# A two-layer decoder trunk on one core: turned pieces of interleaved groups four steps apart

## The chip, the cores and the metric

The kernel runs on one core of one Trainium2 chip. The metric is the device time of one launch in microseconds, the median over runs; lower is better. Engines are named as in the profile: PE multiplies matrices, DVE does vector work, ACT applies functions and scaled copies, POOL and SP here mostly issue DMAs. DMAs are issued from the queues of SP, POOL and ACT, and each engine takes its instructions in order.

## The reference

The input x is 256 tokens by 2048 features, float32. Two layers follow each other, each a mixer and a gated feed-forward net (ffn) with a residual sum after both.

```python
h = rms_norm(x, gain)                                   # before every mixer and ffn
# layer 0, mixer A and B: one projection to u, v, q, f, i, g (1024 each)
u, v = gelu(u), rms_norm_per_head(gelu(v))              # 8 heads of 128
y_a  = u * (tril(sp_w) @ v + sp_b)                      # in chunks of 128 tokens
y_b  = rms_norm_per_head(hgrn2(q, f, i)) * silu(g)      # gated linear recurrence, 8 heads
x    = x + concat(y_a, y_b) @ w_out
# layer 1, mixer C: q, k, v, g (2048 each) and f (16)
q, k = rms_norm_per_head(q), rms_norm_per_head(k)       # 16 heads of 128
c    = cumsum(log_sigmoid(f + b_f))                     # one row of 256 per head
p    = softmax(causal(q @ k.T * 128**-0.5 + c_t - c_s))
x    = x + ((p @ v) * sigmoid(g)) @ w_out
# ffn in both layers, hidden size 5632
z    = causal_conv3(h @ w_up); a, b = split(z)
x    = x + (silu(a) * b) @ w_down
```

All products are to be good to float32.

## The kernel before

**Matmuls and weights.** A float32 product is made of three matmuls of rounded operands. An activation is kept as a rounded half and a rounded remainder side by side; a weight w arrives by a DMA of 512 KB on SP's queue (L195), ACT writes its rounded copy wh (L206) and DVE the remainder wl (L211). Then PE adds high by high (L287), high by low (L288) and low by high (L289), in `project_four`; `project_tok` does the same for weights laid out by token columns (L267 to L269). The contraction runs over 16 tiles of 128 features (KT = 16, "k-tiles"). One weight tile holds two k-tiles of a group of 512 columns; the 12 matmuls on it are called a step here, and a group takes eight steps. There are four w buffers and three each of wh and wl; the ffn has a second set of two each for every other weight.

**Order of the work.** The program is written as a main line of projections, with everything else in generators. `tick()` is called once ahead of every step and moves each running generator one piece on. `start(g)` runs a generator's first piece at once, `after(n, g)` lets it begin n ticks later, and `queue` holds those that wait until fewer than `depth` of its kind run. A scheduler then orders each engine's instructions by their dependences and this program order; some orders are pinned by hand (`behind`, `in_order`). SP's queue thus holds the weights in the order of the steps, with other DMAs in between.

**Turning.** Projections come out with tokens on the partitions. `transposed` (L308 to L314) turns a group of 512 columns: two DVE transposes into `tmp`, then 16 DMAs of 32 KB into the turned tile, eight on SP's queue and eight on POOL's. After a turn, LAG = 6 ticks pass before the result is used. These 32 KB DMAs are the "turned pieces" of a group, tiles `turn` or `zt` in the profile.

**Pairs.** Where a projection begins with activations that are not all ready, two groups are interleaved by `project_pair`, so that the first 12 k-tiles of both come before the last four of either (JOIN = 12):

```python
for part in ((0, JOIN), (JOIN, KT)):
    for w4, ps in ((wa, pa), (wb, pb)):
        project_four(w4, acts, KT, shift=shift, ps=ps, part=part)
```

In steps: a 6, b 6, a 2, b 2. It serves four places: the outputs of both mixers (`w_abo` with activations `ya` and `yb`, `w_co` with `yc`; two more groups follow alone) and the first two groups of `up` in both ffns.

**Mixer A and B.** `w_v` comes first: two groups, with the loads of x and the first norm between them. The sums of squares of the values v (`sumsq`, a mult L353 and a reduce L354 on DVE, four times), the reciprocal root (`rsq`, L345 to L350, with Ln and Exp on ACT) and four multiplies of gv (L495) are written right after the second group. `mixes`, in `queue`, then makes the eight spatial products, one per tick, after three empty ticks. The first x block, the vector pp and the second x block are issued by ACT's queue (`SC.dma_start`, L84 to L86) at the very start, while the first `w_v` parts are on SP's.

**Mixer C.** The first group of queries (`project_tok` on `w_cqkv[0]`) is interleaved with `keys_gate`, which makes the first group of keys and the 16 columns of the gate f in one pass: queries 12 k-tiles, keys 12, queries 4, keys 4. Then `forget` makes the cumulated gate rows: fc on 16 partitions (a scan, L804), written to DRAM as cd (L806) and read back into cb, every row on all partitions, by one POOL DMA of 2 MB (L807). The queries' and keys' `turn` does the norm per head (`sumsq`, `rsq`, a mult L883) and then `transposed`; both are begun by `start`. Attention reads cb and the turned tiles.

The profile's lines L335 and L714 are the first norm's rounded x tile `a` and the low half of a `yb` tile.

Of the kernel before, what the change touches and what calls it, by code (L numbers as in the profile page):

```python
# [8 lines left out]
F32 = mybir.dt.float32  # L9
# [6 lines left out]
P = 128  # L16
# [10 lines left out]
LAST = 7  # L27
WAIT = 2
JOIN = 12
EPS = 1e-6  # L30
WARM = 7
AHEAD = {2: 2, 4: 4, 6: 6}
# [21 lines left out]
def tile_trunk(ctx: ExitStack, tc: tile.TileContext, x, pp_d, cst_d, mlev_d, msk_d,  # L54
# [13 lines left out]
    def nm(base):  # L68
        count[0] += 1
        return f"{base}_{count[0]}"  # L70
# [13 lines left out]
    SC.dma_start(*fetch[0])  # L84
    SC.dma_start(pp[:, 0:C_FFN], pp_d[:, 0:C_FFN])
    SC.dma_start(*fetch[1])  # L86
    V.memset(ones, 1.0)
# [49 lines left out]
    def start(g):  # L137

        if next(g, g) is not g:
            free.append(g)  # L140
# [30 lines left out]
        while flight or queue or free or soon:  # L171
            tick()

    deep = {"pool": None, "turn": 0}

    def in_order(r, key="dma"):
        if key in deep:
# [98 lines left out]
    def project_four(w4, acts, n, k0=0, shift=0, ps=None, part=None):  # L276
        ps = ps or banks_for()
        for k in range(*(part or (0, n)), 2):
            tick()
            lo = (k0 + (k + shift) % n) * P  # L280
            wh, wl = weights(w4[:, :, lo:lo + 2 * P].rearrange("m p c -> p m c"), 1024, 4)
            for T in range(2):
                for i in range(2):
                    a = acts[k + i]
                    ah, al = a[:, T * P:(T + 1) * P], a[:, S + T * P:S + (T + 1) * P]
                    h, l = (view(t, i * P, (2 * P, 4), (1, P)) for t in (wh, wl))
                    PE.matmul(ps[T], ah, h, start=k + i == 0, stop=False)  # L287
                    PE.matmul(ps[T], ah, l, start=False, stop=False)  # L288
                    deep["mm"] = deep["main"] = PE.matmul(ps[T], al, h, start=False, stop=k + i == n - 1)  # L289
        return ps  # L290

    def project_pair(wa, wb, acts, shift=0):
        pa, pb = banks_for(), banks_for()
        for part in ((0, JOIN), (JOIN, KT)):
            for w4, ps in ((wa, pa), (wb, pb)):
                project_four(w4, acts, KT, shift=shift, ps=ps, part=part)
                if part[1] == KT:
                    yield ps

    def output(w, acts, shift=0):  # L300
        yield from project_pair(w[0:4], w[4:8], acts, shift)
# [38 lines left out]
    def rsq(dst, src, n):  # L340
        tag = "sq" if dst.shape[-1] == S else "rm"
        cols = dst.shape[-1] if dst.shape[-1] == S else LANE // math.prod(dst.shape[1:-1])
        m, t = (tp.tile(list(dst.shape[:-1]) + [max(cols, dst.shape[-1])], F32, tag=tag, name=nm(n_))
                [..., 0:dst.shape[-1]] for n_ in ("rm", "rt"))
        V.tensor_scalar(m, src, 1.0 / n, EPS, ALU.mult, ALU.add)  # L345
        act(dst, m, AF.Ln)
        act(dst, dst, AF.Exp, scale=-0.5)
        V.scalar_tensor_tensor(t, dst, -0.5, dst, ALU.mult, ALU.mult)
        V.tensor_tensor(t, t, m, ALU.mult)
        V.scalar_tensor_tensor(dst, t, 1.5, dst, ALU.add, ALU.mult)  # L350

    def sumsq(dst, src, sq):
        V.tensor_tensor(sq, src, src, ALU.mult)  # L353
        V.tensor_reduce(dst, sq.rearrange("p (h d) -> p h d", d=P), AX.X, ALU.add)  # L354
# [65 lines left out]
    def mixer_ab(norm):  # L420
# [61 lines left out]
                        .to_broadcast([P, NH, P]), ALU.mult)  # L482

        ss = hp.tile([P, LANE], F32, tag="ss", name="ss")
        for g in range(2):
            for T in range(2):
                i = (2 * g + T) * 4
                j = hp.tile([P, 512], F32, tag="smk", name=nm("junk"), bufs=1)
                sumsq(ss[:, i:i + 4], gv[g][:, T], j)
        rsq(ss[:, 0:2 * NH], ss[:, 0:2 * NH], P)  # L490
        for g in range(2):
            for T in range(2):
                i = (2 * g + T) * 4
                v4 = gv[g][:, T].rearrange("p (h d) -> p h d", d=P)
                V.tensor_tensor(v4, v4, ss[:, i:i + 4].unsqueeze(2).to_broadcast([P, 4, P]), ALU.mult)  # L495
        mg = [keep("mg") for _ in range(NH)]

        def mix(h):
# [9 lines left out]
                                   ALU.mult, ALU.add)  # L508

        def mixes():  # L510
            yield
            yield
            yield
            for h in range(NH):
                mix(h)
                yield

        queue.append(mixes())


        gam = pp[:, C_GAM:C_GAM + 3 * NH]
# [225 lines left out]
    def mixer_c(norm):  # L747
# [6 lines left out]
        def keys_gate(part):  # L754
            for k in range(*part):
                if k % 2 == 0:
                    tick()
                w = wp.tile([P, n], F32, tag="w", name=nm("w"), bufs=4)
                wh = wp.tile([P, n], F32R, tag="wh", name=nm("wh"), bufs=3)
                wl = wp.tile([P, n], F32R, tag="wl", name=nm("wl"), bufs=3)  # L760
                nc.gpsimd.dma_start(w[:, 0:CH], w_cf[:, k * P:k * P + CH])
                nc.sync.dma_start(w[:, CH:n], w_cqkv[CH // 4][:, k * 512:(k + 1) * 512])
                deep["act"] = SC.activation(wh, w, AF.Copy)
                deep["sub"] = V.tensor_tensor(wl, w, wh.bitcast(F32), ALU.subtract)
                a = norm.a[k]
                for T in range(2):
                    ah, al = a[:, T * P:(T + 1) * P], a[:, S + T * P:S + (T + 1) * P]
                    for j, (a_, t) in enumerate(((ah, wh), (ah, wl), (al, wh))):
                        begin, end = k + j == 0, k == KT - 1 and j == 2
                        PE.matmul(pa[T][:, 0:CH + S], a_, t[:, 0:CH + S], start=begin, stop=end)  # L770
                        deep["main"] = PE.matmul(pb[T][:, 0:S], a_, t[:, CH + S:n], start=begin, stop=end)  # L771

        first = banks_for()
        for part in ((0, JOIN), (JOIN, KT)):
            project_tok(w_cqkv[0], norm, ps=first, part=part)
            keys_gate(part)
        drain()
        depth[0] = 2
        Rt = norm.Rt
# [3 lines left out]

        ct = hp.tile([P, 2, 2 * CH], F32, tag="ct", name="ct")[..., 0:CH]
        cb = hp.tile([P, CH * S], F32, tag="big", name="cb").rearrange("p (h s) -> p h s", s=S)

        def forget():
            f, fa, fc, on = (hp.tile([P, S], F32, tag=t, name=t)[0:CH] for t in ("f", "fa", "fc", "on"))
            ft = hp.tile([P, 2, LANE], F32, tag="ft", name="ft")
            V.memset(on, 1.0)  # L790
            for T in range(2):
                SC.activation(ft[:, T, 0:CH], pa[T][:, 0:CH], AF.Copy, scale=Rt[:, T:T + 1])
            yield
            ps = bank()
# [8 lines left out]
            V.scalar_tensor_tensor(f, f, 0.0, fa, ALU.min, ALU.subtract)  # L803
            V.tensor_tensor_scan(fc, on, f, 0.0, ALU.mult, ALU.add)  # L804
            cd = dp.tile([CH, S], F32, tag="cd", name="cd")
            nc.gpsimd.dma_start(cd, fc)  # L806
            nc.gpsimd.dma_start(cb, cd.partition_broadcast(P))  # L807
# [82 lines left out]
        for g in range(CH // 4):  # L890
            qkv = []
            for j in range(3):
                ps = None if g == 0 and j == 1 else first if g + j == 0 else \
                    project_tok(w_cqkv[j * (CH // 4) + g], norm)
                z = piece("z", 2) if j < 2 else piece("v", 2)
                if ps is None:
                    start(forget())
                for T in range(2):
                    if ps is None:
                        SC.activation(z[:, T, 0:S], pa[T][:, CH:CH + S], AF.Copy, scale=Rt[:, T:T + 1])  # L900
                        SC.activation(z[:, T, S:512], pb[T][:, 0:S], AF.Copy, scale=Rt[:, T:T + 1])
                    else:
                        SC.activation(z[:, T], ps[T], AF.Copy, scale=Rt[:, T:T + 1])
                if j < 2:
                    t = piece("turn", 4)
                    start(turn(z, t))
                    z = heads(t)
                qkv.append(z)
            os_.append(piece("o", CH // 4))
            queue.extend(attend(h, *qkv, os_[g]) for h in range(4 * g, 4 * g + 4))  # L910
# [284 lines left out]
```

## Time and profile before

| | us |
|---|---|
| median of 3 runs | 2319.3 |
| lowest and highest run | 2317.0, 2320.3 |
| the profiled execution, device time | 2317.44 |
| its span in the profile | 2315.7 |
| PE busy | 2292.7 |
| DVE, ACT, POOL busy | 1557.9, 1313.3, 356.5 |

The span is the time from the first to the last recorded work of one execution; the device time of that execution is 1.7 us longer. Times inside the trace count from the start of the span. "Busy" for PE also counts matmuls at a reduced clock: the profile shows the granted clock as PEclk, where 1.00 is full speed. An instruction's row gives its start, its length, engine, line and operation, the tile written and the tile read (`pm<-wh,a`), and in brackets how long its engine stood idle before it and what ended that.

### The profile page before, as it was taken

To read this page: it belongs to the slowest core of one execution; us is meant where nothing else is said; L and a number is where in the kernel's file an instruction comes from. 1 tells how busy PE (TensorE), PEld (TensorE's weight loads), DVE (VectorE), ACT (ScalarE), POOL (GpSimd) and SP (SyncE) were. 2 spreads that over 40 slices of the span, in tenths; PEclk is the share of its full clock that TensorE was granted. 3 is DMA by queue.
4 is the path that set the end of the run, shared out by engine and by line. 5 is a ranking of instruction groups with operands and counts; after the bars stand their busy time and mean duration, and the time that the engine had idled before them with its cause. 6 is when DMAs were issued, how large, how long until landed. Compare 5 with 4: busy or idle time off the path is not lost.

```text
span 2315.7 us, 31427 instructions
## 1 busy us (share of the span) xinstructions
PE 2292.7 (99%) x10370; PEld 1903.9 (82%) x10370; DVE 1557.9 (67%) x2369; ACT 1313.3 (57%) x1953; POOL 356.5 (15%) x661
## 2 busy tenths in 40 slices
PE   9999999999999999999989999999999999999999
PEld 7888887888888888888868888878888888888887
DVE  7788766777566657766756665657777467657666
ACT  7577655665455545654545556646655456456642
POOL 0101121122012002111211101121221022012102
PEclk9999999999999999999999999999999999999999
DMA  8755667777667657776666555767777677667765
GB/s 273 205 186 169 187 204 222 228 235 214 203 204 218 214 185 227 221 215 189 181 198 201 185 187 174 227 207 229 235 219 219 193 213 218 204 203 219 220 204 172
DMA packets 499204, 481.06 MB, mean 208 GB/s; under 512 B 116992, under 2 KB 468368, under 8 KB 498912
## 3 DMA queue, kind: packets, MB, share of 16 engines
q1 hardware_dynamic: 475344, 451.83, 62.5%
q0 software_dynamic: 21248, 23.69, 4.6%
q10 hardware_dynamic: 2448, 3.53, 0.5%
q8 instruction: 81, 1.33, 0.2%
q14 instruction: 83, 0.68, 0.1%
HBM read 434.85 MB, written 2.12 MB: 189 GB/s over the span
## 4 chain that ended last, share of the span: by engine, by line
PE 75%; DMA 2%; DVE 1%; SPq 1%; issue 0%; ACT 0%; DVEq 0%; ACTq 0%; POOLq 0%
PE pm L288 21%; PE pm L289 21%; PE pm L287 21%; PE pm L267 3%; PE pm L268 3%; PE pm L269 3%; SPq L314 1%; DMA zt<-tmp 1%; PE px L161 1%; PE px L770 1%; DMA turn<-tmp 0%; PE pm L771 0%; DVE wl L211 0%; DVE tmp L308 0%; PE px L164 0%
## 5 line engine op out<-in xcount | busy, mean ns | idle before, releaser
L211 DVE TENSOR_TENSOR wl<-w,wh 128x1024 fp32r<-128x1024 f32 (+1 forms) x812 | 986.7, 1218 | 655.6 <-ACT wh L206 650.0
L206 ACT ACTIVATE wh<-w 128x1024 fp32r<-128x1024 f32 (+1 forms) x812 | 854.6, 1054 | 796.3 <-PE pm L289 555.6
L288 PE MATMUL pm<-wl,a 128*128 128x512 f32 x1792 | 698.4, 390 | 2.9 <-DVE wl L211 2.9
L287 PE MATMUL pm<-wh,a 128*128 128x512 f32 x1792 | 701.0, 391 | 0.0
L289 PE MATMUL pm<-wh,a 128*128 128x512 f32 x1792 | 698.1, 390 | 0.0
L314 POOL DMA_DIRECT2D zt<-tmp x413 | 223.7, 549 | 1203.0 <-DVE tmp L308 1000.6
L288 PEld LDWEIGHTS pm<-wl,a 128*128 128x128 f32 x1792 | 336.8, 188 | 73.3 <-DVE wl L211 4.6
L289 PEld LDWEIGHTS pm<-wh,a 128*128 128x128 f32 x1792 | 336.6, 188 | 69.8
L287 PEld LDWEIGHTS pm<-wh,a 128*128 128x128 f32 x1792 | 336.7, 188 | 69.2
L288 PE MATMUL pm<-wl,hid 128*128 128x512 f32 x688 | 267.9, 389 | 0.0
L287 PE MATMUL pm<-wh,hid 128*128 128x512 f32 x688 | 267.9, 389 | 0.0
L289 PE MATMUL pm<-wh,hid 128*128 128x512 f32 x688 | 267.9, 389 | 0.0
L314 POOL DMA_DIRECT2D turn<-tmp x224 | 121.4, 550 | 635.3 <-DVE tmp L308 299.1
L267 PE MATMUL pm<-wh,a 128*128 128x512 f32 x464 | 184.3, 398 | 8.3 <-ACT wh L206 8.3
L268 PE MATMUL pm<-wl,a 128*128 128x512 f32 x464 | 181.9, 392 | 0.2 <-DVE wl L211 0.2
L269 PE MATMUL pm<-wh,a 128*128 128x512 f32 x464 | 181.6, 391 | 0.0
L289 PEld LDWEIGHTS pm<-wh,hid 128*128 128x128 f32 x688 | 129.2, 188 | 26.8
L287 PEld LDWEIGHTS pm<-wh,hid 128*128 128x128 f32 x688 | 129.2, 188 | 26.7
L288 PEld LDWEIGHTS pm<-wl,hid 128*128 128x128 f32 x688 | 129.2, 188 | 26.7
L155 ACT ACTIVATE conv<-zt,pp 128x256 f32<-128x256 f32 x176 | 95.6, 590 | 24.2 <-DMA zt<-tmp 23.0
L267 PEld LDWEIGHTS pm<-wh,a 128*128 128x128 f32 x464 | 87.6, 189 | 26.0 <-ACT wh L206 8.7
L308 DVE STREAM_TRANSPOSE tmp<-z 128x512 f32<-128x512 f32 x132 | 92.2, 706 | 18.4 <-ACT z L974 16.0
(217 smaller groups left out, 1935.3 us busy)
## 6 DMA issues: line engine op xcount, KB each, us to landing
w<-in_w_up SPq DMA_DIRECT2D x352, 512.0 KB, 4.5
w<-in_w_dn SPq DMA_DIRECT2D x176, 512.0 KB, 4.3
w<-in_w_cqkv SPq DMA_DIRECT2D x88, 512.0 KB, 4.3
w<-in_w_abo SPq DMA_DIRECT2D x32, 512.0 KB, 4.4
w<-in_w_cg SPq DMA_DIRECT2D x32, 512.0 KB, 4.0
w<-in_w_co SPq DMA_DIRECT2D x32, 512.0 KB, 4.0
zt<-tmp SPq DMA_DIRECT2D x414, 32.0 KB, 2.4
zt<-tmp POOLq DMA_DIRECT2D x413, 32.0 KB, 2.3
```

The source lines that it names most:

```text
L155: return behind(SC.activation(*args, **kw), "act")
L161: return behind(PE.matmul(*args, **kw), "main")
L206: deep["act"] = SC.activation(wh[:, p], w[:, p], AF.Copy)
L211: deep["sub"] = V.tensor_tensor(wl[:, p], w[:, p], wh[:, p].bitcast(F32), ALU.subtract)
L267: PE.matmul(ps[T], ah, h, start=k + i == 0, stop=False)
L268: PE.matmul(ps[T], ah, l, start=False, stop=False)
L269: deep["main"] = PE.matmul(ps[T], al, h, start=False, stop=k + i == KT - 1)
L287: PE.matmul(ps[T], ah, h, start=k + i == 0, stop=False)
L288: PE.matmul(ps[T], ah, l, start=False, stop=False)
L289: deep["mm"] = deep["main"] = PE.matmul(ps[T], al, h, start=False, stop=k + i == n - 1)
L308: V.transpose(tmp.rearrange("p (b m i t) -> p b m i t", b=4, m=4, t=2)[:, :, :, :, T], src(T).rearrange("p (m b j) -> p b m j", m=4, b=4))
L314: qs[(a + b) % len(qs)].dma_start(dst[BLK * b:BLK * (b + 1), :, a * n:(a + 1) * n], tmp[BLK * a:BLK * (a + 1), b * 4 * n:(b + 1) * 4 * n] ...
```

## The change

It has six parts.

1. The first x block is issued by SP's queue, ahead of the first weights, and takes its place in the chain of pinned DMAs, instead of by ACT's queue.
2. `project_pair` gives the second group eight k-tiles at first (HALF = 8), not 12. In steps: a 6, b 4, a 2, b 4. Group a ends four steps ahead of group b, before it was two.
3. The start of mixer C does the same with the first queries and keys.
4. The values' sums, `rsq` and multiplies become steps of a generator, with a tick between them, and `mixes` goes on from there; it is begun by `after(6, ...)` and no longer counted in `queue`.
5. The gate rows cb are read back in four DMAs of four rows (512 KB) each, four ticks apart.
6. The turn of the first keys begins four ticks later.

```diff
+HALF = 8
...
-    SC.dma_start(*fetch[0])
+    first_dma = nc.sync.dma_start(*fetch[0])
...
-    deep = {"pool": None, "turn": 0}
+    deep = {"pool": None, "turn": 0, "dma": first_dma}
...
     def project_pair(wa, wb, acts, shift=0):
         pa, pb = banks_for(), banks_for()
-        for part in ((0, JOIN), (JOIN, KT)):
-            for w4, ps in ((wa, pa), (wb, pb)):
-                project_four(w4, acts, KT, shift=shift, ps=ps, part=part)
-                if part[1] == KT:
-                    yield ps
+        for w4, ps, part in ((wa, pa, (0, JOIN)), (wb, pb, (0, HALF)), (wa, pa, (JOIN, KT)), (wb, pb, (HALF, KT))):
+            project_four(w4, acts, KT, shift=shift, ps=ps, part=part)
+            if part[1] == KT:
+                yield ps
...
-        for g in range(2):
-            for T in range(2):
-                i = (2 * g + T) * 4
-                j = hp.tile([P, 512], F32, tag="smk", name=nm("junk"), bufs=1)
-                sumsq(ss[:, i:i + 4], gv[g][:, T], j)
-        rsq(ss[:, 0:2 * NH], ss[:, 0:2 * NH], P)
...
+        def values():
+            for g in range(2):
+                for T in range(2):
+                    i = (2 * g + T) * 4
+                    j = hp.tile([P, 512], F32, tag="smk", name=nm("junk"), bufs=1)
+                    sumsq(ss[:, i:i + 4], gv[g][:, T], j)
+                    yield
+            rsq(ss[:, 0:2 * NH], ss[:, 0:2 * NH], P)
+            for g in range(2):
+                for T in range(2):
...
+                    V.tensor_tensor(v4, v4, ss[:, i:i + 4].unsqueeze(2).to_broadcast([P, 4, P]), ALU.mult)
+                yield
...
         def mixes():
-            yield
-            yield
-            yield
+            yield from values()
             for h in range(NH):
                 mix(h)
                 yield
 
-        queue.append(mixes())
+        after(6, mixes())
...
         first = banks_for()
-        for part in ((0, JOIN), (JOIN, KT)):
+        for part, other in (((0, JOIN), (0, HALF)), ((JOIN, KT), (HALF, KT))):
             project_tok(w_cqkv[0], norm, ps=first, part=part)
-            keys_gate(part)
+            keys_gate(other)
...
+        def rows(to, of):
+            nc.gpsimd.dma_start(to, of)
+            yield
...
-            nc.gpsimd.dma_start(cb, cd.partition_broadcast(P))
+            for g in range(4):
+                c = slice(4 * g, 4 * g + 4)
+                after(4 * g, rows(cb[:, c], cd[c].partition_broadcast(P)))
...
-                    start(turn(z, t))
+                    if ps is None:
+                        after(4, turn(z, t))
+                    else:
+                        start(turn(z, t))
```

More of the change, by code (lines that the diff above doesn't have):

```diff
@@ L484, in mixer_ab @@
         ss = hp.tile([P, LANE], F32, tag="ss", name="ss")
-        for g in range(2):
-            for T in range(2):
-                i = (2 * g + T) * 4
-                j = hp.tile([P, 512], F32, tag="smk", name=nm("junk"), bufs=1)
-                sumsq(ss[:, i:i + 4], gv[g][:, T], j)
-        rsq(ss[:, 0:2 * NH], ss[:, 0:2 * NH], P)
[L491 to L495, printed above, removed]
+        def values():
[8 more added lines that the diff above has]
+                for T in range(2):
+                    i = (2 * g + T) * 4
+                    v4 = gv[g][:, T].rearrange("p (h d) -> p h d", d=P)
+                    V.tensor_tensor(v4, v4, ss[:, i:i + 4].unsqueeze(2).to_broadcast([P, 4, P]), ALU.mult)
+                yield
         mg = [keep("mg") for _ in range(NH)]
```

## The prediction

> **What bounds the kernel now.** I read the page's first part, then the windows for the places where PE falls behind, then PE's waits, and last the queues' own timelines there.
>
> ```profile
> span 2315.7 us, 31427 instructions
> PE 2292.7 (99%) x10370; PEld 1903.9 (82%) x10370; DVE 1557.9 (67%) x2369; ACT 1313.3 (57%) x1953; POOL 356.5 (15%) x661
> ```
>
> PE is busy for 99% of the span and the change takes no matmul away, so only PE's losses can be won. Busy time hides some of them: a matmul at half clock counts as busy. I therefore count matmuls against an undisturbed stretch (columns: stretch, length, busy us and number of each engine, granted clock, DMA share, GB/s).
>
> ```profile
> core 0: us, PE busy (x) PEld busy (x) DVE busy (x) ACT busy (x) POOL busy (x), PEclk, DMA share, GB/s
> 500.00:750.00 250.00, 250.00 (x1105) 207.10 (x1104) 160.09 (x209) 139.69 (x184) 39.01 (x72) 1.00 0.69 210
> 48.00:62.00 14.00, 12.83 (x56) 9.91 (x56) 12.73 (x27) 11.67 (x16) 1.05 (x1) 1.00 0.52 156
> 350.00:365.00 15.00, 12.48 (x47) 9.55 (x46) 8.14 (x15) 8.17 (x14) 0.00 (x0) 0.89 0.79 247
> 455.00:466.00 11.00, 10.27 (x45) 8.16 (x45) 11.00 (x22) 8.19 (x14) 4.00 (x8) 1.00 0.46 133
> 1180.00:1200.00 20.00, 11.69 (x39) 8.79 (x38) 7.53 (x14) 7.41 (x14) 2.97 (x6) 0.74 0.64 208
> 1550.00:1565.00 15.00, 13.12 (x50) 10.03 (x49) 7.08 (x13) 7.23 (x13) 1.86 (x4) 0.89 0.84 251
> 1558.30:1561.60 3.30, 3.30 (x9) 2.56 (x8) 3.10 (x6) 1.96 (x4) 0.00 (x0) 0.50 0.95 294
> ```
>
> 250/1105 = 0.2262 us is one matmul, and 12 of them, 2.72 us, one step (two k-tiles). A stretch's loss is its length less 0.2262 times its matmuls: 14 - 56 x 0.2262 = 1.3 at 48, 4.4 at 350, 0.8 at 455, 11.2 at 1180, 3.7 at 1550. (A few matmul records may be missing, so each is good to some tenths.) At 1558.3 the clock is 0.50 after a stall, so a stall costs more than its idle time.
>
> ```profile
> PE pm L267 <- ACT wh L206: 8.3, 1, 8.3
> 1556.73 0.50 PE L287 MATMUL pm<-wh,yc 128*128 128x512 f32 x1 [1.35 <-ACT wh L206]
> ```
>
> The largest wait, 8.3 us at once (total, times, longest), is for a rounded weight at 1180; of the 11.2 there the other 2.9 are half clock. ACT had nothing to round, as SP's queue and POOL's timeline show (start, us, instruction):
>
> ```profile
> 338.19 11.80 SPq L314 DMA_DIRECT2D turn<-tmp  x16
> 350.10 6.59 SPq L195 DMA_DIRECT2D w<-in_w_abo  x5
> 1168.65 16.12 SPq L314 DMA_DIRECT2D turn<-tmp  x16
> 1184.87 6.52 SPq L195 DMA_DIRECT2D w<-in_w_cqkv  x5
> 1540.46 11.16 SPq L314 DMA_DIRECT2D turn<-tmp  x16
> 1551.73 8.39 SPq L195 DMA_DIRECT2D w<-in_w_co  x6
> 1166.92 0.56 POOL L807 DMA_DIRECT2D cb<-cd  x1 [2.02 <-DMA cd<-fc]
> 1178.08 4.89 POOL L314 DMA_DIRECT2D turn<-tmp  x9 [5.38 <-DMA turn<-tmp]
> 1169.29 11.01 DMA turn<-tmp
> w<-in_w_cqkv SPq DMA_DIRECT2D x88, 512.0 KB, 4.3
> turn<-tmp SPq DMA_DIRECT2D x224, 32.0 KB, 2.1
> cb<-cd POOLq DMA_DIRECT2D x1, 2048.0 KB, 10.9
> ```
>
> SP issues in order, weights included. At 338, 1540 and 1168 two groups' turned pieces (8 + 8) stand back to back, and no weight is issued for 11.8, 11.2 and 16.1 us: more than four steps (10.9 us), what the four w buffers cover. At 1168 there is more: a piece took 11.01 us where the median is 2.1, beside the 2 MB gate rows, issued 1166.92 and 10.9 us long; SP and POOL stood behind it.
>
> **The change part by part.**
>
> *Outputs (w_abo, w_co).* The two interleaved groups end four steps apart, not two. In the changed order SP issues 8 pieces, three weights, 8 pieces. Half of 11.8 is 5.9 us, two steps, inside what four buffers cover. I take the stalls as gone but 0.2 each: -4.2 and -3.5 (ends: all gone, -4.4 and -3.7; nothing gained, 0). No DMA is added here. The first group's last four activations are wanted two steps earlier:
>
> ```profile
> L287 PE MATMUL pm<-wh,yb x64: 388/389/629, 309.4 to 390.0; 128*128 128x512 f32 x64
> L714 DVE SCALAR_TENSOR_TENSOR yb<-turn,pp,yb x16: 427/436/447, 287.4 to 313.4; 128x128 fp32r<-128x128 f32 x16
> ```
>
> In w_abo the yb tiles are the last eight of 16. The first group takes the first four in two steps from 309.4, the second group's four steps follow, and the last four are wanted at 309.4 + 6 x 2.72 = 325.7. The last is written at 313.4 + 0.4 = 313.8: 11.9 us spare, no cost.
>
> *Start of mixer C.* Queries and keys' groups also end four steps apart; the keys' turn comes four ticks later; the gate rows go in four DMAs. SP: 8 query pieces, five weights, 8 key pieces. POOL: 8 query pieces, the gate row's cd, two parts, 8 key pieces, two parts; so the query pieces pass ahead of the broadcast, and the key pieces meet 1 MB (half of 10.9, 5.4 us) instead of 2. The three added issues are 3 x 0.56 = 1.7 us of a POOL busy for 15%. The old 11.2 goes. What is late next is DVE: in the new order these stand between the third split (wl) and the fourth of the next group (durations from before, other order):
>
> ```profile
> 1162.14 0.40 DVE L803 SCALAR_TENSOR_TENSOR f<-f,fa 16x256 f32<-16x256 f32 x1
> 1162.47 0.67 DVE L353 TENSOR_TENSOR junk<-z 128x512 f32<-128x512 f32 x1
> 1163.14 0.67 DVE L804 TENSOR_TENSOR_SCAN fc<-on,f 16x256 f32<-16x256 f32 x1
> 1163.74 0.65 DVE L354 TENSOR_REDUCE ss<-junk 128x4 f32<-128x512 f32 x1
> 1165.80 0.17 DVE L345 TENSOR_SCALAR rm<-ss 128x8 f32<-128x8 f32 x1
> 1165.92 1.29 DVE L883 TENSOR_TENSOR z<-z,ss 128x512 f32<-128x512 f32 x2
> 1167.13 0.16 DVE L348 SCALAR_TENSOR_TENSOR rt<-ss 128x8 f32<-128x8 f32 x1
> 1167.20 0.70 DVE L308 STREAM_TRANSPOSE tmp<-z 128x512 f32<-128x512 f32 x1
> 1168.55 1.21 DVE L211 TENSOR_TENSOR wl<-w,wh 128x1024 fp32r<-128x1024 f32 x1
> ```
>
> 0.40 + 0.67 + 0.67 + 0.65 + 0.17 (rm), a round trip to ACT for Ln and Exp (rm to rt is 1.33 with mults between: I take 0.7), three small ones 0.5, 1.29, 0.70 and the split 1.21: 7.0, less some 0.4 because starts lie closer than durations: 6.6 us. The first split must end as the first step begins; up to the third stand two splits, a small add, one junk and one reduce, 2 x 1.21 + 0.17 + 0.67 + 0.65 = 3.9, so the fourth ends at 3.9 + 6.6 = 10.5. PE wants it after three steps and the fourth's first matmuls, 3 x 2.72 + 1.0 = 9.2. A new gap of 1.3, then; the nearest row is 1.35 at 1556.73, followed by half clock over 3.3 us, which costs half of that, 1.6. New loss 2.9, net -8.3. Ends: 0 (sums run ahead; -11.2) and 8.2 (gap doubled to 2.6; two late parts make the next weight 2.7 late, half of 5.4; half clock 2.9 as at 1180; -3.0). I take 2.9 because the broadcast's late parts have loaded weights ahead of them. [...]
>
> *up(0), both ffns.* The same turn; before, 0.8 is lost at 455 where the two groups' convolutions fill DVE (11.00 of 11). Four steps apart they overlap less, but fall among later ones: -0.4 (ends -0.8, +0.8).
>
> *Values' sums.* As generator steps they keep nearly their place on DVE; the rsq and the four multiplies go about 12 steps later, and ACT gets two more table loads:
>
> ```profile
> L97 ACT ACT_TABLE_LOAD x19 | 24.4, 1283 | 2.5 <-issue 2.1
> ```
>
> 2 x 1.28 = 2.6 us on an engine 57% busy, hidden by two waiting rounded tiles; multiplies of some 0.65 each join DVE later. The 1.3 at 48 comes from sums that stay. 0 (ends -1.3; +1.5, about one load uncovered).
>
> *First x block on SP instead of ACT.*
>
> ```profile
> 0.74 0.86 SPq L195 DMA_DIRECT2D w<-in_w_v  x2
> 0.73 0.42 ACTq L84 DMA_DIRECT2D x<-in_x  x1
> 1.18 0.45 ACTq L85 DMA_DIRECT2D pp<-in_pp  x1
> 5.23 0.35 DVE L335 TENSOR_SCALAR a<-x,pp 128x256 fp32r<-128x256 f32 x1 [4.22 <-DMA pp<-in_pp]
> ```
>
> ACT's pp goes 0.45 earlier and SP's weights 0.43 later. The first activation waits for pp, so it may gain, until the later weight takes over: -0.2 (ends -0.6, +0.2).
>
> Sum: -4.2 - 3.5 - 8.3 - 0.4 + 0 - 0.2 = -16.6. Against the profiled execution, 2317.4: 2300.8. That execution stands 1.9 below the median of 2319.3, so 2302.7 on the scale of the runs; I say 2302.5.
>
> **Rivals.**
>
> *Nothing new at mixer C's start.* DVE's sums fit between splits and the 11.2 goes whole: -4.2 - 3.5 - 11.2 - 0.6 = -19.5, 2299.8. For it: the scheduler may be run ahead by idle DVE (7.53 busy of 20 there). Against: DVE runs in order, and the round trip stands ahead of the fourth split.
>
> *A long new stall there*, the 8.2 above: -4.2 - 3.5 - 3.0 - 0.6 = -11.3, 2308.0. For it: a piece behind a broadcast took 11.01 us. Against: parts are a quarter as large, and weights stood on another queue. [...]
>
> *Pairs still late.* Three weights between two lots of pieces are too few, and both outputs keep their stalls: -8.3 - 0.6 = -8.9, 2310.4. For it: the weights that follow 1551.73 still take 8.39 for six. Against: 8 pieces are half the hole.
>
> *Slower: the earlier use of the last four activations.* In five places (both outputs, both up(0), mixer C's start) PE would reach acts 12 to 15 two steps, 5.4 us, earlier. If they come 3.0 late each time, each costs 3.0 and 1.6 of half clock: 23, and -16.6 + 23 = +6.4, 2325.7. From 2.6 late in all five it is slower by 0.2%. Against: by the rows above they would have to come 11.9 us later in w_abo to be late at all.
>
> **How the numbers follow.** Forecast 0.56, nothing new 0.17, long stall 0.13, pairs late 0.06, slower 0.08. A measurement of this kernel tells about 0.2% (4.6 us) from no change. Long stall and pairs late still lie beyond it (11.3 and 8.9); to mixtures of them, with part of the slower one, goes 0.06 within: faster 0.86, same 0.06, slower 0.08. The range: all terms at their best, -4.4 - 3.7 - 11.2 - 0.8 - 1.3 - 0.6 = -22.0, 2297.3, less the 2.3 by which the lowest run lies under the median: 2295; above, pairs late 2310.4 and a little run scatter: 2312.
>
> **What would show it.** In the windows about 350 and 1550 the lost time under 0.5 and a clock of 1.00; in SP's timeline `turn<-tmp x8` with weights between instead of x16. At mixer C's start no PE wait near 8 us, key pieces well under 11 us, four cb rows of 512 KB, and a gap of about 1.3 named for wl. At 48 and 455 no more than about today's losses; 21 table loads with no PE wait beside them. It is wrong if PE waits for yb, yc or A tiles, if weights still come late at the pairs, or if a broadcast part now holds weights.

## The result

The changed kernel takes 2304.7 us (median of 4 runs, 2301.5 to 2308.9) against 2318.2 for the kernel before; the ratio is 0.9944, 95% interval 0.9923 to 0.9964. Measured again beside other kernels it was 2306.4, ratio 0.9962 (0.9948 to 0.9976). The forecast was 2302.5 in a range of 2295 to 2312. The execution that was profiled, and that all rows of "after" below come from, took 2308.89, the slowest of the four. Line numbers are up to twelve higher than before (L206 is L207, L211 is L212), and some are the same (L308, L314).

First the page's span and busy times of the changed kernel:

```profile
span 2307.1 us, 31430 instructions
PE 2289.0 (99%) x10370; PEld 1899.5 (82%) x10370; DVE 1559.8 (68%) x2369; ACT 1313.3 (57%) x1955; POOL 358.3 (16%) x664
```

Then the windows at the places that the prediction named (columns as there), with two more, at 30 and 72:

```profile
30.00:40.00 10.00, 9.23 (x40) 7.01 (x39) 6.94 (x11) 5.68 (x11) 0.00 (x0) 1.00 0.72 231
48.00:62.00 14.00, 12.72 (x56) 9.84 (x55) 12.57 (x24) 11.49 (x13) 0.90 (x1) 1.00 0.46 142
72.00:76.00 4.00, 2.55 (x10) 1.58 (x9) 2.04 (x2) 2.11 (x2) 0.56 (x1) 1.00 0.94 229
350.00:365.00 15.00, 14.63 (x64) 11.76 (x64) 10.83 (x20) 8.62 (x14) 1.02 (x2) 1.00 0.76 229
455.00:466.00 11.00, 11.00 (x49) 8.93 (x48) 8.50 (x10) 4.67 (x6) 4.33 (x8) 1.00 0.84 229
1160.00:1172.00 12.00, 11.03 (x49) 8.57 (x48) 8.57 (x15) 4.43 (x6) 4.92 (x9) 1.00 0.76 260
1172.00:1190.00 18.00, 15.45 (x60) 12.03 (x59) 6.34 (x6) 7.87 (x9) 2.19 (x4) 0.91 0.92 287
1550.00:1565.00 15.00, 12.97 (x49) 9.99 (x48) 11.95 (x20) 10.51 (x16) 0.38 (x1) 0.89 0.85 251
```

Length less 0.2262 us for each matmul gives the lost time: 0.5 at 350 (4.4 before), none at 455 (0.8), 0.9 + 4.4 = 5.3 at mixer C's start (11.2), but 3.9 at 1550 (3.7), still 1.3 at 48, and two new losses, 1.7 at 72 and 1.0 at 30. The differences are -3.9, -0.8, -5.9, +0.2, 0, +1.7 and +1.0, together -7.7; 2317.4 - 7.7 = 2309.7, near the 2308.9 of this execution.

PE's timeline of the changed kernel at the remaining losses (start, us, instruction, in brackets the idle time and what ended it):

```profile
73.95 0.49 PE L288 MATMUL pm<-wh,a 128*128 128x512 f32 x1 [0.68 <-ACT wh L207]
1165.09 0.50 PE L269 MATMUL pm<-wl,a 128*128 128x512 f32 x1 [0.97 <-DVE wl L212]
1180.55 0.73 PE L268 MATMUL pm<-wh,a 128*128 128x512 f32 x2 [2.03 <-ACT wh L207]
1181.81 0.79 PE L269 MATMUL pm<-wl,a 128*128 128x512 f32 x1 [0.53 <-DVE wl L212]
1551.83 0.50 PE L288 MATMUL pm<-wh,yc 128*128 128x512 f32 x1 [1.28 <-ACT wh L207]
1553.09 0.50 PE L289 MATMUL pm<-wl,yc 128*128 128x512 f32 x1 [0.76 <-DVE wl L212]
```

The 8.3 us wait is gone. A gap of 0.97 for a split and a wait of 2.03 for a late weight stand in its place.

SP's timeline shows the two outputs side by side, and why one was mended and the other not:

```profile
335.54 5.10 SPq L314 DMA_DIRECT2D turn<-tmp  x8
340.74 1.63 SPq L196 DMA_DIRECT2D w<-in_w_abo  x3
346.42 5.11 SPq L314 DMA_DIRECT2D turn<-tmp  x8
...
1527.40 5.11 SPq L314 DMA_DIRECT2D turn<-tmp  x8
1532.62 2.79 SPq L196 DMA_DIRECT2D w<-in_w_co  x3
1541.20 5.10 SPq L314 DMA_DIRECT2D turn<-tmp  x8
1546.41 16.57 SPq L196 DMA_DIRECT2D w<-in_w_co  x9
```

In both, the second group's pieces come as eight after three weights. In w_abo they start 10.9 us after the first group's, in w_co 13.8. SP stands in order before 1541.20 and has nothing to issue, because tmp isn't turned yet. POOL's and DVE's timelines of the changed kernel tell why:

```profile
1531.68 2.71 POOL L314 DMA_DIRECT2D turn<-tmp  x5 [2.39 <-issue]
1540.12 0.43 DVE L159 TENSOR_TENSOR x<-x,turn 128x256 f32<-128x256 f32 x1 [2.99 <-DMA w<-in_w_co]
1540.46 0.71 DVE L308 STREAM_TRANSPOSE tmp<-z 128x512 f32<-128x512 f32 x1
```

After three of the first group's pieces POOL was held for 2.39 us by nothing that the profile names ("issue"). The other five pieces then went out together with three weights. DVE's first sum into x (L159), which needs all pieces of that group, waited 2.99 us, and behind it, in order, stood the second transpose of the second group. The row names a weight, which the sum doesn't read; the last of the five late pieces landed at 1539.55.

At mixer C's start the chain that ended last runs over two weights:

```profile
1165.06 7.22 DMA w<-in_w_cqkv
1174.73 4.63 DMA w<-in_w_cqkv
```

The first took 7.22 us (median of w_cqkv 4.4 in this kernel, 4.3 in the one before) beside two parts of the gate rows, and the next was issued only when that one had been rounded and split. By the prediction it should have been covered.

### The profile page after: what moved, and what is told of

The parts are those of the page before. It is cut to its first block, busy times and chain, and to the rows that moved or that the text cites. A ratio compares the mean times of both kernels' runs of the same rounds, so it can differ in the third digit from the quotient of the medians.

```text
span 2307.1 us, 31430 instructions
## 1 busy us (share of the span) xinstructions
PE 2289.0 (99%) x10370; PEld 1899.5 (82%) x10370; DVE 1559.8 (68%) x2369; ACT 1313.3 (57%) x1955; POOL 358.3 (16%) x664
## 3 DMA queue, kind: packets, MB, share of 16 engines
HBM read 434.85 MB, written 2.12 MB: 189 GB/s over the span
## 4 chain that ended last, share of the span: by engine, by line
PE 91%; DMA 4%; DVE 2%; ACT 2%; issue 1%; SPq 1%; POOL 0%; DVEq 0%; ACTq 0%
PE pm L289 26%; PE pm L290 25%; PE pm L288 25%; PE pm L269 4%; PE pm L270 4%; PE pm L268 4%; PE px L162 1%; DVE wl L212 1%; ACT wh L207 1%; DMA w<-in_w_cqkv 1%; DMA w<-in_w_abo 1%; DMA w<-in_w_f 1%; DMA w<-in_w_v 0%; DMA w<-in_w_co 0%; SPq L314 0%
## 5 line engine op out<-in xcount | busy, mean ns | idle before, releaser
L212 DVE TENSOR_TENSOR wl<-w,wh 128x1024 fp32r<-128x1024 f32 (+1 forms) x812 | 985.8, 1218 | 653.2 <-ACT wh L207 649.0
L207 ACT ACTIVATE wh<-w 128x1024 fp32r<-128x1024 f32 (+1 forms) x812 | 854.2, 1054 | 798.1 <-PE pm L290 563.2
L314 POOL DMA_DIRECT2D zt<-tmp x413 | 223.7, 549 | 1201.8 <-DVE tmp L308 993.9
L289 PEld LDWEIGHTS pm<-wl,a 128*128 128x128 f32 x1792 | 336.5, 188 | 74.1 <-DVE wl L212 5.1
L288 PEld LDWEIGHTS pm<-wh,a 128*128 128x128 f32 x1792 | 336.5, 188 | 70.4 <-ACT wh L207 1.1
L290 PEld LDWEIGHTS pm<-wh,a 128*128 128x128 f32 x1792 | 336.3, 188 | 70.1
L314 POOL DMA_DIRECT2D turn<-tmp x224 | 121.5, 550 | 634.1 <-DVE tmp L308 267.4
L269 PEld LDWEIGHTS pm<-wl,a 128*128 128x128 f32 x464 | 87.7, 189 | 23.1 <-DVE wl L212 5.7
L308 DVE STREAM_TRANSPOSE tmp<-z 128x512 f32<-128x512 f32 x132 | 92.3, 706 | 20.1 <-ACT z L986 18.1
```

The costliest lines, as they stand in the source:

```text
L207: deep["act"] = SC.activation(wh[:, p], w[:, p], AF.Copy)
L212: deep["sub"] = V.tensor_tensor(wl[:, p], w[:, p], wh[:, p].bitcast(F32), ALU.subtract)
L308: V.transpose(tmp.rearrange("p (b m i t) -> p b m i t", b=4, m=4, t=2)[:, :, :, :, T], src(T).rearrange("p (m b j) -> p b m j", m=4, b=4))
L314: qs[(a + b) % len(qs)].dma_start(dst[BLK * b:BLK * (b + 1), :, a * n:(a + 1) * n], tmp[BLK * a:BLK * (a + 1), b * 4 * n:(b + 1) * 4 * n] ...
```

## The experiments

Each ran beside the kernel before on the same chip, whose medians there were 2315.9 to 2317.0. The edits are shown shortened; a line in words stands for the code of that part in the diff above.

### The outputs' part alone

```diff
 before
+HALF = 8
-project_pair: wa 0-12, wb 0-12, wa 12-16, wb 12-16
+project_pair: wa 0-12, wb 0-8, wa 12-16, wb 8-16
```

> The kernel before with part 2 alone (project_pair: wa 12, wb 8, wa 4, wb 8 k-tiles). Theory: the late weights at both outputs come from two groups' pieces back to back on SP, so the loss about 350 us (4.4) falls under 1; at w_co it goes too unless POOL's hold of 2.2 to 2.4 us falls among the first group's pieces. That hold stood at POOL's 430th instruction in both profiles; without the added broadcast issues it should fall after the sixth of the first group's eight pieces, so that two pieces are late instead of five, and the loss at 1550 is 0 to 4. Mixer C's start keeps its 11 to 12. Time 2309 to 2314. Rival (the hold is chance): it falls elsewhere, and the loss at 1550 is under 1, 2309.

Measured: 2306.8 (2306.4 to 2307.2), ratio 0.9957 (0.9942 to 0.9972). That is 9.4 us under the kernel before, as much as the whole change gained when it was measured the second time (9.6). Windows and POOL's timeline of this kernel:

```profile
350.00:365.00 15.00, 14.79 (x66) 11.90 (x65) 11.97 (x22) 10.33 (x18) 0.00 (x0) 1.00 0.86 271
1172.00:1195.00 23.00, 16.30 (x67) 12.48 (x66) 8.18 (x16) 11.83 (x25) 4.58 (x9) 0.85 0.65 208
1545.00:1565.00 20.00, 19.05 (x84) 15.20 (x83) 15.11 (x25) 12.18 (x20) 3.28 (x7) 1.00 0.81 251
1532.39 1.09 POOL L314 DMA_DIRECT2D turn<-tmp  x2 [2.18 <-issue]
```

At 350 nothing is lost, and at 1550 only 20 - 84 x 0.2262 = 1.0, with the hold where the expectation put it, after the sixth piece: two pieces are late, not five. At mixer C's start 7.8 is still lost in the second window. Its time lies below the expected 2309 to 2314, since that loss and smaller ones also came out lower than in the profile of before; of these I have no cause.

### Mixer C's start alone

```diff
 before
+first queries and keys 12, 8, 4, 8 k-tiles
+cb in four DMAs, after(4 * g)
+first keys' turn by after(4)
```

> The kernel before with parts 3, 5 and 6 alone (mixer C's start). Theory: the wait of 8.3 goes and in its place come a DVE gap of about 1.0 and a late weight of 2 with half clock, as in the changed kernel's profile; loss between 1150 and 1200 some 7 instead of 12.6; outputs keep 4 to 5 each. Time 2311 to 2315. Rival (the new stalls there come from what the other parts delay): loss there under 3, 2308 to 2310.

Measured: 2310.7 (2307.9 to 2315.3), ratio 0.9975 (0.9965 to 0.9984). The new gaps at mixer C's start come with this part itself: PE waits 1.06 for a split, then 0.50, 0.53, 0.68 and 0.76 us for late weights and their splits between 1181 and 1187. The waits for late weights are smaller than in the changed kernel, and no half clock followed: the loss between 1160 and 1200 is 4.3, where some 7 was expected.

### Part 4 alone, and undone

```diff
 before
+values() in steps, mixes() by after(6)
```

> The kernel before with part 4 alone (values in steps, mixes by after). Theory: od is issued 1 to 2 us later against PE's work, its 11 to 13 us of slow transfers then reach into the next group's weights, and a loss of 2 to 5 us appears at 73 where the kernel before has none; everything else as before, 2317 to 2321. Rival (the loss at 73 needs the first x block on SP too): none at 73, 2315 to 2317.

Measured: 2319.5 (2313.4 to 2321.8), ratio 1.0009 (0.9999 to 1.0019): not told apart from no change by the interval, but the loss is there, in PE's timeline:

```profile
74.70 0.50 PE L287 MATMUL pm<-wh,a 128*128 128x512 f32 x1 [2.74 <-ACT wh L206]
```

```diff
 changed
-values() in steps, mixes() by after(6)
+sums, rsq and multiplies at once; mixes() in queue
```

> The changed kernel with part 4 undone (values' sums, root and multiplies right after the second group; mixes in queue). Theory: the moved values let the small vectors behind the 4 KB write od come 2.2 us later, that write slows every transfer beside it for 11 to 12 us, and a weight issued meanwhile is late by 1.5: the loss of 2 us at 73 goes, table loads are 19, time 2301 to 2304. Rival (the first x block on SP shifts the loads there): the loss at 73 stays, time 2303 to 2306.

Measured: 2301.0 (2299.9 to 2306.3), ratio 0.9937 (0.9920 to 0.9954). No PE wait above 0.1 us is left between 60 and 140. So part 4, which I had costed at nothing, costs 2.5 us by the one comparison of medians and 3.7 to 5.3 by the other (2304.7 and 2306.4 less 2301.0). These last compare different chips, and the half clocks that the changed kernel's profile shows at 1181 and 1554 are missing in this one's, so not all of them need be part 4's. But the parts add up without it: on this chip, against 2316.2, the outputs' part gave 9.4, mixer C's 5.5, and all parts but part 4 15.2. The loss at 72 to 76 stood in every kernel with part 4 and od's old write, and in none without part 4: 0.6 to 3.5 us of idle in the seven profiles, with half clock after it in four.

### What is slow at 61 to 73: od as rows

od is the 8 x 128 table of 1 - lb, written to DRAM by POOL as 1024 single numbers and read back by orow. Here PE turns it first.

```diff
 changed
-nc.gpsimd.dma_start(od.rearrange("h p -> p h"), omlb)
+odt = hp.tile([P, P], F32, tag="odt", name="odt")[0:NH]
+ops_ = bank()
+turn_in(ops_[0:NH, 0:P], omlb, ident)
+V.tensor_copy(odt, ops_[0:NH, 0:P])
+nc.gpsimd.dma_start(od, odt)
```

> The changed kernel with od made by a PE transpose and one copy, so that its 4 KB go out as eight rows of 512 bytes instead of 1024 single numbers. Theory: the write of single numbers fills the DMA engines for 11 to 12 us and the weights beside it take as long; as rows it lands in 2 to 4 us, the weights near it in 4 to 5, and the loss of 2 at 73 goes; 1.5 to 3 us under the changed kernel. Rival (the loads of weights themselves or the values' place on DVE make them late): od lands early but the weights near 61 to 73 still take 8 us or more and the loss stays.

Measured: 2299.8 (2298.6 to 2302.1), ratio 0.9935 (0.9918 to 0.9952), the fastest of all. DMA issues between 55 and 80 us, first of the changed kernel, then of this one (last column: median us from issue to landing):

```profile
w<-in_w_q SPq DMA_DIRECT2D x6, 512.0 KB, 8.1
w<-in_w_f SPq DMA_DIRECT2D x2, 512.0 KB, 7.8
od<-gm POOLq DMA_DIRECT2D x1, 4.0 KB, 11.8
```

```profile
w<-in_w_q SPq DMA_DIRECT2D x6, 512.0 KB, 4.5
w<-in_w_f SPq DMA_DIRECT2D x2, 512.0 KB, 4.4
od<-odt POOLq DMA_DIRECT2D x1, 4.0 KB, 4.3
```

A write of 4 KB slowed the weights beside it to nearly half speed (8.1 and 7.8 us) for 11.8 us; as eight rows it lands in 4.3 and they take 4.4 to 4.5. The kernel before has the same slow write (12.0 us) and loses nothing by it: it issues it at 58.9 us, the changed kernel at 61.1, and the one with part 4 alone at 59.8. That this shift of 1 to 2 us is what lets the slow stretch reach a weight that PE needs is argued from the order, not tried by itself. This run also lost nothing at 1550: POOL's hold came after the second piece of w_co's second group (2.45 us before 1535.56). A sum waited 1.23 us there too, but no transpose stood right behind it. At mixer C's start PE waited only 0.37 + 0.53 us, without half clock (more on this below). So its gain over the changed kernel, 4.9 to 6.5 us by medians, is that of three places, and not od's alone.

### POOL's hold

```diff
 changed
+spare = dp.tile([4, NH], F32, tag="spare", name="spare")
+for i in range(4):
+    nc.gpsimd.dma_start(spare[i:i + 1], cst[0:1, i * NH:(i + 1) * NH])
```

> The changed kernel with four DMAs of 32 bytes added on POOL's queue at the start; nothing else moves. Theory: POOL is held some 2.3 us at every 106th instruction (111, 217, 430, 536, 642 in the profiles); four more ahead move the hold at w_co from before the fourth piece of the first group to a piece of the gates before it, which has some 7 us to spare. Loss at 1550 from 4.2 to under 1, time 2299 to 2302. Rival (the hold is chance or comes from weights on the DMA engines): the hold stays at the same piece or moves without rule, time as the changed kernel, 2301 to 2309 by run.

Measured: 2306.4 (2305.6 to 2307.2), ratio 0.9956 (0.9941 to 0.9970). POOL's timeline and the window:

```profile
1531.42 3.25 POOL L314 DMA_DIRECT2D turn<-tmp  x6 [2.45 <-issue]
1550.00:1565.00 15.00, 14.58 (x65) 11.73 (x64) 13.59 (x21) 10.47 (x17) 3.74 (x7) 1.00 0.83 251
```

The hold moved, but by one piece (six follow it, not five), not by four: it stood after POOL's instruction 433, in the changed kernel after 430, so a count of instructions alone doesn't place it. The loss at 1550 fell to 15 - 65 x 0.2262 = 0.3, since this time the sum waited 1.18 us, not 2.99. The time didn't fall, because the start lost more: 1.04 and 0.73 us of idle at 33 and 37, where the changed kernel lost 0.77 and its repetition nothing. There DVE stood in order for loads of pp and wt, 4.08 and 0.75 us here, 0.81 and 2.70 in the changed kernel, 2.13 and 0.42 in its repetition. These differ from run to run, but the four added DMAs were issued at 21.3 to 23.0, beside those loads, and may have delayed them; no run tells the two apart. Of the expectation the loss at 1550 came true, the size of the shift and the time didn't.

### The sums behind the transposes

```diff
 changed, add_four
-after(LAST if q == 3 else LAG, rest())
+after(LAST if q == 3 else LAG + (q == 0), rest())
```

> The changed kernel with the sums of the outputs' first group begun one tick later, so that on DVE both transposes of the second group stand ahead of the first x sum. Theory: at w_co that sum waits for pieces which POOL's hold made late, the second transpose behind it is 3 to 4 us late, and with it the pieces on SP and the weights behind them. With the transposes first the loss at 1550 falls from 4.2 to under 1, whatever POOL does; about 4 us under the changed kernel. Rival (three weights between the lots of pieces are too few): the loss stays at 3 to 4.

Measured: 2304.9 (2300.5 to 2308.5), ratio 0.9953 (0.9938 to 0.9968). POOL, DVE and the window of this kernel:

```profile
1533.97 2.71 POOL L314 DMA_DIRECT2D turn<-tmp  x5 [2.39 <-issue]
1539.82 0.71 DVE L308 STREAM_TRANSPOSE tmp<-z 128x512 f32<-128x512 f32 x1 [0.41 <-ACT z L402]
1542.06 0.42 DVE L159 TENSOR_TENSOR x<-x,turn 128x256 f32<-128x256 f32 x1
1545.00:1565.00 20.00, 20.00 (x89) 16.32 (x88) 18.41 (x33) 14.71 (x25) 2.28 (x5) 1.00 0.73 225
```

The hold is in the same place, the second transpose now stands ahead of the sum, and PE is busy for all 20 us. This decides the cause at w_co: a late sum in front of the transpose. Three weights between the lots of pieces are enough. The medians don't show the 4 us: against the changed kernel's repetition on the same chip (`after2` below) they differ by 1.5 us, the profiled executions by 3.0. The loss at 73 was 2.75 + 0.64 us of idle in this profile, 2.12 + 0.46 in that one, both with half clock after it.

### The gate rows

Whole again:

```diff
 changed
-for g in range(4): after(4 * g, rows(cb[:, c], ...))
+nc.gpsimd.dma_start(cb, cd.partition_broadcast(P))
```

> The changed kernel with part 5 undone: cb again by one DMA of 2 MB, ahead of the first keys' pieces on POOL. Theory: what the parts bought is that the key pieces wait behind 1 MB instead of 2; whole, the pieces take 9 to 12 us, the weight behind them is later, and the loss at mixer C's start grows from 7 to 10 to 12. POOL's hold falls after the sixth piece at w_co, so the loss at 1550 falls from 4 to some 1.5. Together 0 to 3 us over the changed kernel, 2305 to 2309. Rival (the four steps between the turns do it, the parts nothing): loss at mixer C's start 7, time 2 to 3 us under the changed kernel.

Measured: 2307.4 (2306.1 to 2308.9), ratio 0.9958 (0.9944 to 0.9971). PE's timeline, and the DMA issues between 1155 and 1185:

```profile
1180.34 0.73 PE L268 MATMUL pm<-wh,a 128*128 128x512 f32 x2 [1.99 <-ACT wh L207]
cb<-cd POOLq DMA_DIRECT2D x1, 2048.0 KB, 10.5
turn<-tmp SPq DMA_DIRECT2D x10, 32.0 KB, 9.1
```

The wait is 1.99, in four parts it was 2.03. At w_co nothing was lost, with POOL's hold after the sixth piece; the time isn't lower, since PE's wait at 73 was 2.19 in this profile. On mixer C's start the rival holds: as part 5 put them, four parts gained nothing here; the four steps between the turns did it (parts 3 and 6, which no run separates).

Behind the keys' pieces (`behind(..., "turned")` pins a part behind the last turned piece on POOL's queue):

```diff
 changed
-after(4 * g, rows(...))                 nc.gpsimd.dma_start(to, of)
+after(4 * g + 6, rows(...))             behind(nc.gpsimd.dma_start(to, of), "turned")
```

> The changed kernel with the gate rows' four DMAs issued behind the first keys' pieces on POOL (three right behind, the fourth behind the next queries' pieces). Theory: the late weight at 1178 stood on SP behind key pieces that took 9 us beside the first two parts; with the parts behind them the pieces land in 2 to 4 us and the loss at mixer C's start falls from 7 to about 3 (the gap of 1.0 on DVE stays); 3 to 4 us under the changed kernel run beside it. Rival (the five weights and DVE are what is late there): loss stays at 6 to 7.

Measured: 2305.6 (2300.2 to 2308.8), ratio 0.9954 (0.9939 to 0.9970). My theory fell: the key pieces, but for the last (6.54), now landed in 2 to 4 us and the next weight was issued at 1172.22 instead of 1174.73, yet PE's wait grew. PE's timeline and the chain:

```profile
1181.78 0.73 PE L268 MATMUL pm<-wh,a 128*128 128x512 f32 x2 [2.49 <-ACT wh L207]
1172.22 8.37 DMA w<-in_w_cqkv
```

Three parts went out within 1.6 us beside that weight, and it took 8.37. It was the first of four weights issued within 2.6 us, which took 8.37 to 9.79; the four issued together at 1157.31, before any part, had taken 3.86 to 5.64. So what stood beside gate rows was late, pieces (7.0 us by median beside 1 MB in the changed kernel) or weights (8.37 to 9.79 beside 1.5 MB here). So they were spread, one part for each group of heads, and the two other mends added:

```diff
 changed, with od as rows and LAG + (q == 0)
-after(4 * g, rows(...))                 nc.gpsimd.dma_start(to, of)
+after(20 * g + 6, rows(...))            behind(nc.gpsimd.dma_start(to, of), "turned")
```

> The changed kernel with od written as rows, the sums of the outputs' first group one tick later, and the gate rows' four DMAs spread: the first behind the first keys' pieces, each other one behind a later group's. Theory: the losses at 73 and 1550 go (2 to 6 and 4), and with one part of 512 KB instead of three beside it the weight at 1172 lands in 5 to 6 us instead of 8.4, so the loss at mixer C's start falls from 6 or 7 to 3 or 4. Time 2294 to 2298. Rival (the late weight there is set by the pieces ahead of it on SP): mixer C's start stays at 6, time 2297 to 2300.

Measured: 2302.1 (2299.7 to 2303.2), ratio 0.9933 (0.9920 to 0.9947), a miss by 4 us. PE's timeline and a window:

```profile
1176.04 0.73 PE L268 MATMUL pm<-wh,a 128*128 128x512 f32 x2 [0.37 <-ACT wh L207]
1172.00:1190.00 18.00, 17.11 (x75) 13.53 (x74) 8.11 (x7) 10.01 (x13) 0.00 (x0) 1.00 0.78 263
```

The late weight at mixer C's start is nearly gone: 0.37 + 0.53 idle, 18 - 75 x 0.2262 = 1.0 lost instead of 4.4, and the loss at 73 is gone too. But the spreading is not shown to have done this. The kernel with od as rows alone, which issues its gate rows as the changed kernel does, waits no longer there (SP, POOL and PE):

```profile
1161.17 0.33 SPq L196 DMA_DIRECT2D w<-in_w_cqkv  x1
1161.72 1.10 POOL L795 DMA_DIRECT2D cb<-cd  x2 [4.70 <-DMA cd<-fc]
1175.02 0.73 PE L268 MATMUL pm<-wh,a 128*128 128x512 f32 x2 [0.37 <-ACT wh L207]
```

In it the weight went out 0.55 us ahead of the first part and landed in 3.93 us. In the seven other profiles with gate rows from this place it went out 0.2 to 0.5 us behind the first part; its landing and PE's later wait rose roughly together: 4.92 and 0.50 (mixer C's start alone), 6.30 and 1.12 (part 4 undone), 7.22 and 2.03 (the changed kernel), 8.50 and 1.99 (gate rows whole). So some tenths of a us in the order of one weight and the first part go with 1.7 us of wait. In this kernel the later sums now meet other DVE work at w_co (0.58 and 0.35 idle), and od's turn on PE waited 0.79 at 58. The kernel with od as rows alone, 2299.8, wasn't beaten.

With part 4 undone besides:

> The same with part 4 undone as well (values' sums as in the kernel before). Theory: the values' place cost time only through od's slow write, which is gone in both, so this one and the one with part 4 agree within 1.5 us. Rival (the moved multiplies and the two table loads cost by themselves): this one is 2 us or more faster.

Measured: 2304.1 (2301.3 to 2304.8), ratio 0.9940 (0.9928 to 0.9953). It is not faster without part 4; the medians differ by 2.0, more than the 1.5 expected, the other way from the rival. So the two table loads and the moved multiplies cost nothing that shows, and part 4's price came through od alone.

The changed kernel once more, unedited:

> The changed kernel again, nothing edited. Losses that its program makes stay: 2 at 73, about 7 at mixer C's start, 4 at 1550 with POOL's hold after the third piece. Losses of chance move: the 0.8 at 34, which comes from a load of wt that landed after 8.7 us. 2301 to 2309. Rival (all of it chance): the losses at 73 and 1550 are gone in this profile.

Measured: 2306.4 (2302.5 to 2311.5). PE's wait for a weight at 74 was 2.12 us (0.68 in the first profile), those at 1180 1.56 and 0.53, those at 1553 0.78 and 0.76, the hold again after the third piece, and the idle time at 34 was gone. So the first three are the program's, with a size that varies, and the last is chance.

## Why the prediction was right

The time came out 2 to 4 us above 2302.5, and the sign held. Of the mechanisms, w_abo, up(0) and DVE's gap at mixer C's start held; w_co, the broadcast at mixer C's start and the values' sums did not. That the number lies so near is in part luck. The gain was 13.4 us by medians, 9.6 the second time, of 16.8 forecast, and the terms below come to -7.7, less than half of -16.6. The forecast was taken from a median of 2319.3, where the kernel before later had 2315.9 to 2318.2; and the profiled execution is the slowest of four, so which losses the faster ones lacked isn't seen. Point by point, in the terms of the sum against the profiled execution:

- **w_abo**, -4.2: -3.9. Right, and its activations yb cost nothing early.
- **w_co**, -3.5: +0.2. Wrong. The step that failed is "half of 11.8 is 5.9 us, two steps, inside what four buffers cover": it counted SP's issue time alone. What is late next was DVE's sum, standing between the second group's transposes and waiting for pieces that POOL's hold had delayed. A hold of 2.18 us among w_co's pieces was already in the profile of before (POOL, 1544 to 1546: `1546.16 1.09 POOL L314 DMA_DIRECT2D turn<-tmp  x2 [2.18 <-issue]`), and should have made me ask what stands behind a late piece on DVE. The rival "pairs still late" came true in one of two places, by another road than three weights being too few.
- **Mixer C's start**, -8.3: -5.9. The old wait went, and the DVE gap was sized well, 0.97 against 1.3. Two steps failed. The half clock that was added to this gap (1.6) didn't follow it (granted clock 1.00 from 1160 to 1172). And "the broadcast's late parts have loaded weights ahead of them" was wrong: a weight beside two parts took 7.22 us, and the next was 2.03 late, with half clock after it. The end that I named for it, two parts making a weight 2.7 late, was the nearer one. In the kernels that place the gate rows in other ways, what stood beside 1.5 to 2 MB of them was late too: pieces took 9.1 us beside the whole 2 MB, a weight 8.37 beside three parts; which weight it hits, and how hard, hung on tenths of a us.
- **up(0)**, -0.4: -0.8, the better end.
- **Values' sums**, 0 (to +1.5): +1.7 at 72 in this profile, 3.7 to 5.3 us by medians. Wrong: I weighed ACT and DVE and not what follows on POOL's queue. The small vectors behind od, which I hadn't listed as moved, came later, and with them a transfer beside which weights took 7.8 to 8.1 us, not 4.4 to 4.5.
- **First x block**, -0.2: not told apart in the time, as the start's other losses vary by more than that from run to run. PE's first real matmul began at 5.69 instead of 5.73; over all profiles it began at 5.48 to 5.73 in the ten kernels with part 1 and at 5.73 to 6.26 in the four without, which fits the term.

The 1.0 at 30 was in no term.

The gap of 0.97 cost only itself, and the 2.03 + 0.53 us idle at 1180 were followed by half clock (0.91 over the 18 us). Weights weren't held behind a broadcast, but one took 7.22 us beside two parts and one 8.37 beside three, where the kernel before has a median of 4.3: a price that I took as nothing.

## What to carry to other kernels

When two bursts on one queue are pulled apart, follow what the second burst waits for on every engine, not only how long the queue is free: here one late sum in front of a transpose undid the gain in one of two equal places. Weights took 4.9 to 9.8 us and pieces up to 11.0 beside 1 to 2 MB of gate rows, where the medians before are 4.3 and 2.1, and moving the rows changed which of them was late; look at which transfer is issued some tenths of a us before or behind it. Spreading it along the time until it is needed suggests itself, but the one kernel that did so was not faster. Write small tables to DRAM in rows: here 4 KB as single numbers took 11.8 us and the weights beside them 7.8 to 8.1, as eight rows 4.3 and 4.4 to 4.5, and whether that cost anything seems to have hung on a shift of 1 to 2 us in its start.

## What the runs showed of the hardware

- POOL's queue of DMAs is held for 2.2 to 2.45 us at intervals, by nothing that the profile names: in the kernel before for 2.36, 2.36, 2.18 and 2.44 us after its instructions 111, 217, 430 and 642, in the changed kernel for 2.36, 2.36, 2.39 and 2.23 us after 111, 217, 430 and 536, multiples of some 106 apart. The changed kernel's three more broadcast parts left it at 430, but four DMAs of 32 bytes moved it by only one piece, to 433, and od as eight rows instead of 1024 numbers moved it to 437 (2.45 us in both). What holds it wasn't tried.
- The half clock hung on more than the length of a wait: it followed 1.35 + 0.53 us of idle at w_co in the kernel before, and didn't follow 2.49 + 0.53 at mixer C's start with the gate rows behind the pieces. In all fourteen traces the granted clock changes only at points that lie whole multiples of 3.41 us apart, and half clock, before the end of the program, lasts one, two or three such stretches: in the kernel before it begins at 356.77, 1186.21 and 1558.27, 243 and 109 times 3.41 apart, and lasts 3.41, 10.24 and 3.41 us, in the changed kernel at 1181.74 and 1553.80, 109 times 3.41 apart, for 3.41 us each. Between two points PE's idle time (length less PE busy) can be added up. Two stretches of the kernel before, then two with the gate rows behind the pieces:

```profile
1554.85:1558.26 3.41, 1.53 (x6) 0.67 (x5) 1.55 (x2) 1.91 (x2) 0.00 (x0) 1.00 1.04 347
1558.26:1561.68 3.42, 3.42 (x9) 2.66 (x9) 3.19 (x7) 2.00 (x4) 0.00 (x0) 0.50 0.95 294
1177.71:1181.12 3.41, 1.57 (x7) 0.95 (x6) 0.00 (x0) 1.14 (x2) 0.00 (x0) 1.00 1.00 378
1181.12:1184.54 3.42, 2.24 (x9) 1.57 (x10) 2.49 (x3) 3.13 (x4) 0.00 (x0) 1.00 0.75 255
```

  In the first both waits fell into one stretch, 1.88 us of idle; in the second a point split them, 1.84 and 1.18. Of all stretches at full clock between 9 us and PE's last matmul, the 11 with over 1.9 us of idle were all followed by half clock, of the 9 with 1.5 to 1.9 us five were, and none with less (in the kernel before 2.26 us at 353 were followed by it, in the changed kernel 2.48 at 1178 and 2.03 at 1550, but not 1.44 at 72). So the prediction, which set the half clock beside the 1.35 us of idle at 1556.73, left out the 0.53. The points lie elsewhere in each execution (one at 1181.74 in the changed kernel, at 1183.66 in its repetition), so whether a wait of 2 us costs 1.7 us more is in part chance.
